# Stages of 256 tokens that begin on features not yet divided by their rms

## The chip, the cores and the metric

The kernel runs on one core of a Trainium2 chip. The metric is the device time of one execution in microseconds (us). Times are given of the profiled execution where a trace is read, and as medians where kernels are compared.

## The reference

A first block of two layers works on 256 tokens `x` and, in its first layer, on 256 context tokens as well; a second block of two layers works on the 256 tokens alone. The width is 1024. Every stage begins with an rms norm over the 1024 features of a token, times a weight that is put together from the norm's gain and a scale, plus a shift:

```python
def rms_norm_2(x, g):
    xf = x.astype(jnp.float32)
    y = xf * lax.rsqrt(jnp.mean(xf * xf, axis=-1, keepdims=True) + EPS)
    return (y * g.astype(jnp.float32)).astype(x.dtype)

def modulate_2(x, shift, scale):
    return x * (1 + scale[:, None, :]) + shift[:, None, :]

def sqrelu_mlp(hn, w1, w2):
    return jnp.square(jax.nn.relu(hn @ w1)) @ w2

def conv_ffn(h, w_up, conv_w, conv_b, w_down):      # first block
    a = h @ w_up
    a = lax.conv_general_dilated(a, conv_w, ...) + conv_b     # 3 taps, per feature
    gate, val = jnp.split(a, 2, axis=-1)
    return (jax.nn.silu(gate) * val) @ w_down

def second_block(x, c, ...):
    h = x
    for layer in range(DEPTH):
        sh1, sc1, g1, sh2, sc2, g2 = ...
        hn = modulate_2(rms_norm_2(h, norm1_g[layer]), sh1, sc1)
        y = recurrent_mixer(hn, ...) if layer < N_A_LAYERS else chunk_attention(hn, ..., k_pad, v_pad)
        h = h + g1[:, None, :] * y
        hn = modulate_2(rms_norm_2(h, norm2_g[layer]), sh2, sc2)
        h = h + g2[:, None, :] * sqrelu_mlp(hn, mlp_w1[layer], mlp_w2[layer])
        if layer == N_A_LAYERS - 1:
            k_pad, v_pad = shared_kv(h, c_act, ...)  # keys and values, from a norm of their own
    return h
```

## The kernel before

**Layout.** Activations lie with features on the partitions: `x` is 8 tiles (`KD`) of 128 features by 256 tokens (`T`), and a matrix of weights is used as blocks of 128 by 128. A product of fp32 precision is made of three fp32r matmuls in `mm3` (lines 338 to 340): both operands are split into a high and a low part, and wh·hi, wh·lo and wl·hi are summed in PSUM. `load_w` (line 306) brings a block of 128 by 1024 weights: SP issues the DMA into `st`, ACT casts the high part `wh` (line 311), DVE subtracts for the low part `wl` (line 315). `st`, `wh` and `wl` turn in 6 buffers, so the cast of the seventh block waits until TensorE has finished with the first.

**Order.** The program is written as Python code that a scheduler puts in order, by priorities, for every engine but TensorE, whose order is that of the code. Each engine then works through its own list in order. What stands in a list is the same in every execution.

**The hand-offs.** Where one stage ends and the next begins on 256 tokens, the norm stands between. There are five such places behind the first layer, called H1 to H5 here: H1 from the output matrix of the mixer (`wo`) to the conv FFN (`ffn1`), H2 from its last sums (`da`) to the recurrent layer (`lru_layer`), H3 from that layer's last sums (`da`) to the first MLP (`mlp`), H4 from the MLP's last sums to the attention (`attn_layer`, whose first products are `dt`: keys, then queries, then values), H5 from the attention's output matrix (`db`) to the second MLP. At each of them:

1. As one of the 8 output tiles leaves PSUM, DVE adds it to `x` (line 472), ACT squares it (lines 400 and 404), DVE sums the squares (line 405).
2. After the last, TensorE sums over the partitions (`nps`, line 416), DVE takes the root in nine small steps (lines 419 and 289 to 302, up to `nbc`), and TensorE transposes the result (`npt`, line 426). A few matmuls without use (`warm`, line 274) stand in between.
3. `norm_k` (line 445) makes each of 8 tiles of normalised features: DVE `nt` = x times 1/rms (line 447), ACT the high part (line 448), ACT or DVE the same again unrounded (`nhf`, lines 451 and 453), DVE or POOL the low part (line 454). The parts are named by their stage: `h21h`, `h21l` at H1, `lhh`, `lhl` at H2, `m0h`, `m0l` at H3, `kvh`, `kvl` and `hqh`, `hql` at H4, `m1h`, `m1l` at H5.
4. `lead_b` (line 1205) runs four matrices at once through the 8 tiles, tile by tile, into banks `ld`: 96 matmuls. What follows takes a matrix at a time (`pair_b`, line 1216, `up` in the recurrent layer), into `up`.

**What comes of the products.** In the MLPs two matrices make one pair: `evac` (line 1253) takes Relu and square on ACT and the square's low part on DVE. The down matrices (`da`) begin six pairs behind (`LAG_MLP`), which here means after eight up matrices; they sum into four PSUM banks over the whole stage (`DownAcc`, line 495 on), the last three (`LAG_MLP[1]`) held back and run one output tile after another. In `ffn1` a pair is gate and value of the conv FFN (`glu`, line 1076), and `da` begins after five pairs. In the recurrent layer `sink_x` (line 1320) makes the conv, `xh` on ACT (line 1327), `xl` on POOL (line 1328); the gates (`gt`) take these, and from them runs a long chain of ACT, DVE and POOL work and a scan.

## Time and profile before

| | before |
|---|---|
| median of 3 runs | 1752.1 us (1749.39 to 1755.54) |
| profiled execution | 1752.06 us, of which span 1750.3 us |
| TensorE busy | 1634.3 us (93%) |
| VectorE (DVE) busy | 1343.4 us (77%) |
| ScalarE (ACT) busy | 888.1 us (51%) |
| GpSimd (POOL) busy | 179.6 us (10%) |
| chain of waits, share by engine | PE 71%, DVE 8%, ACT 3% |

PE is the matmuls, PEld TensorE's loads of weights, which overlap them. A matmul's own duration is longer than its share of a dense stream, since matmuls overlap; the pace is read from one start to the next. A granted clock of 1.00 is full speed. In a timeline row the bracket gives the idle time of the engine ahead of the instruction, and what ended it. The execution lasts 1.8 us longer than its span.

### The profile page before, as it was taken

To read this page: it belongs to the slowest core of one execution; us is meant where nothing else is said; L and a number is where in the kernel's file an instruction comes from. 1 tells how busy PE (TensorE), PEld (TensorE's weight loads), DVE (VectorE), ACT (ScalarE), POOL (GpSimd) and SP (SyncE) were. 2 spreads that over 40 slices of the span, in tenths; PEclk is the share of its full clock that TensorE was granted. 3 is DMA by queue.
4 is the path that set the end of the run, shared out by engine and by line. 5 is a ranking of instruction groups with operands and counts; after the bars stand their busy time and mean duration, and the time that the engine had idled before them with its cause. 6 is when DMAs were issued, how large, how long until landed. Compare 5 with 4: busy or idle time off the path is not lost.

```text
span 1750.3 us, 28553 instructions
## 1 busy us (share of the span) xinstructions
PE 1634.3 (93%) x10850; PEld 1413.9 (81%) x10850; DVE 1343.4 (77%) x2589; ACT 888.1 (51%) x1526; POOL 179.6 (10%) x247
## 2 busy tenths in 40 slices
PE   6997989999999998987999998897999999899999
PEld 3774459888888886844899997896999977499999
DVE  5868757689999957876689777887888887668553
ACT  4537555542333435565565555765544464655442
POOL 2220220000000001102000001432000011400000
PEclk9999989999999998998899998998999989999999
DMA  9316436246878533152557553456888843668552
GB/s 335 105 48 218 169 124 209 102 138 199 273 224 312 187 111 101 61 181 108 181 197 249 184 180 104 129 180 198 291 318 323 299 152 121 217 241 277 187 186 73
DMA packets 91354, 327.91 MB, mean 187 GB/s; under 512 B 10064, under 2 KB 11088, under 8 KB 90704
## 3 DMA queue, kind: packets, MB, share of 16 engines
q1 hardware_dynamic: 90928, 323.99, 54.7%
q0 software_dynamic: 288, 2.10, 0.3%
q8 instruction: 85, 1.39, 0.3%
q14 instruction: 53, 0.43, 0.1%
HBM read 325.00 MB, written 1.05 MB: 186 GB/s over the span
## 4 chain that ended last, share of the span: by engine, by line
PE 71%; DVE 8%; ACT 3%; issue 3%; POOL 2%; DMA 1%; POOLq 0%; DVEq 0%; ACTq 0%
PE up L339 10%; PE up L338 10%; PE up L340 10%; PE da L338 5%; PE da L339 5%; PE da L340 5%; DVE wl L315 3%; PE dn L338 2%; PE dn L340 2%; PE dn L339 2%; PE dt L544 2%; PE dt L542 2%; PE dt L543 2%; PE opb L648 1%; PE gv L353 1%
## 5 line engine op out<-in xcount | busy, mean ns | idle before, releaser
L311 ACT CAST wh<-st 128x1024 fp32r<-128x1024 f32 (+3 forms) x392 | 401.2, 1030 | 449.7 <-PE up L339 173.4
L315 DVE TENSOR_TENSOR wl<-st,wh 128x1024 fp32r<-128x1024 f32 (+3 forms) x392 | 470.5, 1207 | 139.8 <-ACT wh L311 132.8
L386 DVE CUSTOM_DVE_ANT_0 gst<-gst,crow,cols 128x1024 f32<-128x1024 f32 x128 | 163.6, 1283 | 31.2 <-DMA gst<-in_ada21t_dram 14.4
L338 PE MATMUL up<-h2h,wh 128*128 128x512 f32 (+1 forms) x384 | 143.3, 373 | 1.7 <-ACT h2h L448 1.2
L340 PE MATMUL up<-h2h,wl 128*128 128x512 f32 (+1 forms) x384 | 143.0, 372 | 1.3 <-DVE wl L315 1.3
L338 PE MATMUL da<-g2h,wh 128*128 128x256 f32 x512 | 144.1, 281 | 0.0
L339 PE MATMUL da<-g2l,wh 128*128 128x256 f32 x512 | 144.1, 281 | 0.0
L340 PE MATMUL da<-g2h,wl 128*128 128x256 f32 x512 | 144.1, 281 | 0.0
L339 PE MATMUL up<-h2l,wh 128*128 128x512 f32 (+1 forms) x384 | 143.0, 372 | 0.1
L339 PEld LDWEIGHTS da<-g2l,wh 128*128 128x128 f32 x512 | 96.7, 189 | 0.0
L340 PEld LDWEIGHTS da<-g2h,wl 128*128 128x128 f32 x512 | 96.7, 189 | 0.0
L338 PEld LDWEIGHTS da<-g2h,wh 128*128 128x128 f32 x512 | 96.7, 189 | 0.0
L339 PE MATMUL up<-h21l,wh 128*128 128x256 f32 x320 | 90.1, 281 | 0.0
L340 PE MATMUL up<-h21h,wl 128*128 128x256 f32 x320 | 90.0, 281 | 0.0
L338 PE MATMUL up<-h21h,wh 128*128 128x256 f32 x320 | 90.0, 281 | 0.0
L338 PEld LDWEIGHTS up<-h2h,wh 128*128 128x128 f32 x384 | 72.4, 188 | 15.0 <-ACT h2h L448 1.5
L340 PEld LDWEIGHTS up<-h2h,wl 128*128 128x128 f32 x384 | 72.4, 189 | 14.4 <-DVE wl L315 1.9
L339 PEld LDWEIGHTS up<-h2l,wh 128*128 128x128 f32 x384 | 72.4, 189 | 12.8 <-DVE h2l L454 0.3
L353 PE MATMUL gv<-gst,cst 128*32 128x512 f32 x320 | 59.1, 617 | 20.9 <-DMA gst<-in_w_ada_dram 16.2
L641 POOL TENSOR_SCALAR pf<-pf,rc 128x512 f32<-128x512 f32 (+2 forms) x80 | 43.1, 551 | 195.7 <-DVE rc L959 129.8
L340 PE MATMUL up<-m0h,wl 128*128 128x256 f32 x224 | 63.1, 282 | 0.0
L338 PE MATMUL up<-m1h,wh 128*128 128x256 f32 x224 | 63.0, 281 | 0.0
(542 smaller groups left out, 4780.2 us busy)
## 6 DMA issues: line engine op xcount, KB each, us to landing
st<-in_mlp_dram SPq DMA_DIRECT2D x128, 512.0 KB, 4.5
gst<-in_w_ada_dram SPq DMA_DIRECT2D x96, 512.0 KB, 4.4
st<-in_w_up_dram SPq DMA_DIRECT2D x88, 512.0 KB, 4.4
st<-in_w_in_dram SPq DMA_DIRECT2D x32, 512.0 KB, 3.6
gst<-in_ada20t_dram SPq DMA_DIRECT2D x32, 512.0 KB, 5.1
gst<-in_ada_dram SPq DMA_DIRECT2D x32, 512.0 KB, 4.4
gst<-in_ada21t_dram SPq DMA_DIRECT2D x32, 512.0 KB, 6.2
st<-in_w_down_dram SPq DMA_DIRECT2D x25, 512.0 KB, 3.6
```

Of the source, the lines that this page charges most:

```text
L311: S.copy(hi[:, :n], st[:, :n])
L315: eng.tensor_tensor(lo[:, :n], st[:, :n], f(hi[:, :n]), ALU.subtract)
L338: TE.matmul(ps, lhsT=wh, rhs=ah, start=first, stop=False, **kw)
L339: TE.matmul(ps, lhsT=wh, rhs=al, start=False, stop=False, **kw)
L340: TE.matmul(ps, lhsT=wl, rhs=ah, start=False, stop=last, **kw)
L353: TE.matmul(ps[32 * t:32 * t + 32, :], lhsT=cst[:, 2 * q + i, :], rhs=st[:, i * 512:i * 512 + 512], start=(q < 2), stop=(q >= 2), tile_pos ...
L386: V.tensor_tensor_reduce(o, st, r, 0.5, bias[:, b:b + 1], ALU.mult, ALU.add, dest[:, v, b:b + 1])
L542: TE.matmul(o, lhsT=hh[:, k, js], rhs=wh[:, wsl], start=(k == 0), stop=False)
L543: TE.matmul(o, lhsT=hh[:, k, js], rhs=wl[:, wsl], start=False, stop=False)
L544: TE.matmul(o, lhsT=hlo[:, k, js], rhs=wh[:, wsl], start=False, stop=(k == KD - 1))
L641: G.tensor_scalar(ap, ap, r[:, qt:qt + 1], 0.0, ALU.mult, ALU.add)
L648: TE.matmul(o[c, :], lhsT=vs[x](kt), rhs=PT[:, x, kt].rearrange("p a b -> p (a b)"), start=(kt == 0), stop=(kt == nkt - 1), tile_position= ...
```

## The change

A class `Ahead` takes the place of the norm at the five hand-offs. As an output tile leaves PSUM, ACT writes x times the weight of the norm, `xgh`, and DVE its low part `xgl`; the squares are summed on POOL. TensorE goes straight on to the four first matrices of the next stage with these. The operand has two more columns (258 in place of 256) that hold the shift, so that the product of the matrix and the shift comes out in column 256. `nps` stands between tiles 3 and 4 of the lead, `npt` between tiles 6 and 7 (`RSTD_AT`). ACT copies the transposed 1/rms to `rb`. As a matrix leaves PSUM (`leave`), DVE copies the shift's product (`ldc`) and multiplies the rest by 1/rms (`ldu`); ACT adds the one to the other (`full`, or as the bias of the MLP's Relu, which then takes 256 columns twice in place of 512 once). The two matrices behind the lead (numbers 4 and 5, `AHEAD`) are done in the same way (`more`). `norm_k` still makes all 8 tiles, for the matrices behind those; the warm matmuls of these hand-offs are gone.

At H4 the first half of the keys is made from `xgh` with the tokens on the output's partitions, so 1/rms is a number for each partition there; the shift's product comes from eight small matmuls `gv` on the raw weights, and one more that sums and spreads it. Besides, the sums of a stage lie otherwise in the banks (output tile m in bank m % 4), the tiles leave in the order 0 to 7, the MLPs hold back two down matrices in place of three, and the output goes out in other parts. The core of the diff:

```diff
-OUT_PARTS = ((0, 2, 4, 6), (1, 3, 5), (7,))
+OUT_PARTS = ((0, 1, 2, 3), (4, 5, 6), (7,))
...
-LAG_MLP = (6, 3)
+LAG_MLP = (6, 2)
+AHEAD = 6
+RSTD_AT = (4, 7)
...
+    class Ahead:
+        def __init__(self, x, gs, sh, norm_step=None):
+            self.x, self.gs, self.sh = x, gs, sh
+            self.sums = Sums(G)
...
+        def add(self, k):
+            hi, lo = [t[:, k, 0:T] for t in self.h]
+            S.activation(hi, self.x[:, k, :], AF.Identity, scale=self.gs[:, k:k + 1])
+            V.scalar_tensor_tensor(lo, self.x[:, k, :], self.gs[:, k:k + 1], f(hi), ALU.mult, ALU.subtract)
+            self.sums.add(self.x[:, k, :])
+
+        def lead(self, ws, hi, lo, offset=TAIL_PRIO):
+            bs = [da_bank(j) for j in range(4)]
+            for k in range(KD):
+                if k == RSTD_AT[0]:
+                    with tc.high_priority(offset=TAIL_PRIO):
+                        r = Rstd(self.sums.parts)
+                if k == RSTD_AT[1]:
+                    with tc.high_priority(offset=TAIL_PRIO):
+                        pt = r.done()
+                        self.rb = tl("rb", [T], F32, None, 1, "xg")
+                        S.copy(self.rb, pt)
+                self.mm(k, ws, bs)
+            us = [self.leave(b) for b in bs]
+            with tc.high_priority(offset=offset):
+                for k in range(KD):
+                    norm_k(k, self.x[:, k, :], self.rb, self.gs, self.sh, hi(k), lo(k))
+            return us
...
+        def leave(self, b):
+            with tc.high_priority(offset=PRIO):
+                c = st_("ldc", [1])
+                V.tensor_copy(c, b[:, T:T + 1])
+                u = tl("ldu", [T], F32, "ldu", 4, "xg")
+                V.tensor_tensor(u, b[:, 0:T], self.rb, ALU.mult)
+            return u, c
+
+        def full(self, uc):
+            S.activation(uc[0], uc[0], AF.Identity, bias=uc[1])
+            return uc[0]
...
         def ps(self, m):
-            return self.bk[m // 2][:, m % 2, :]
+            return self.bk[m % 4][:, m // 4, :]
...
-                for m in (0, 2, 4, 6, 1, 3, 5, 7):
+                for m in range(KD):
...
         def make(m):
             if m == 0:
-                ws = [load_w(I["mlp1"][layer, j]) for j in range(4)]
-                for j, b in enumerate(lead_b(ws, hi, lo, norm_step)):
+                us = ahead.lead([load_w(I["mlp1"][layer, j]) for j in range(4)], hi, lo)
+                for j in range(2):
                     with tc.high_priority(offset=LEAD_PRIO):
-                        evac(2 * j, b)
+                        evac(2 * j, us[2 * j:2 * j + 2])
             if m not in parts:
-                evac(m, pair_b([load_w(I["mlp1"][layer, m + j]) for j in range(2)], hi, lo))
+                ws = [load_w(I["mlp1"][layer, m + j]) for j in range(2)]
+                evac(m, ahead.more(ws) if m < AHEAD else pair_b(ws, hi, lo))
...
+        ka = keys_ahead()
+        next(ka)
         norms(gk, kvm[:, 0:8], kv)
-        blk(0, kv, post_kq("kn2", 0))
+        blk(1, kv, post_kq("kn2", 1), ka)
         norms(gq, mod[:, 0:8], hq)
-        blk(1, kv, post_kq("kn2", 1))
```

TensorE's list at H5, from the last product of the attention's output to the first of the MLP. Before:

```order
L340 MATMUL db<-mx2h,wl 128x256
L416 MATMUL nps<-ones_78,acc 128x2 x6
L274 MATMUL warm<-wz 128x256 x2
L426 MATMUL npt<-kc,nbc 128x128 x2
L274 MATMUL warm<-wz 128x256 x3
L338 MATMUL ld<-m1h,wh 128x256
```

TensorE's list at the same place now, around `npt` (four banks `da` of the lead in place of `ld`):

```order
L342 MATMUL da_16816<-xgh,wl 128x258
L340 MATMUL da_16817<-xgh,wh 128x258
L341 MATMUL da_16817<-xgl,wh 128x258
L342 MATMUL da_16817<-xgh,wl 128x258
L428 MATMUL npt<-kc,nbc 128x128 x2
L340 MATMUL da_16814<-xgh,wh 128x258
L341 MATMUL da_16814<-xgl,wh 128x258
```

The lead no longer stands behind `npt`; 84 of its 96 matmuls, which read `xgh` and `xgl`, stand ahead of it.

ACT's list at H5, around the last tiles of normalised features (`m1h`, `nhf`). Before, the last of them, the Relu of the lead (`mr`), its square (`g2h`) and the next weights:

```order
L448 ACTIVATE m1h<-nt,n_91,gs 128x256
L451 ACTIVATE nhf<-nt,n_91,gs 128x256
L448 ACTIVATE m1h<-nt,n_91,gs 128x256
L451 ACTIVATE nhf<-nt,n_91,gs 128x256
L311 CAST wh<-st 128x1024
L1257 ACTIVATE mr<-ld 128x512 x2
L1258 ACTIVATE g2h<-mr 128x512 x2
L311 CAST wh<-st 128x1024 x5
```

Now, from the second Relu of the lead to the last tile of normalised features:

```order
L1323 ACTIVATE mr<-ldu,ldc 128x256
L1326 ACTIVATE g2h<-mr 128x512
L453 ACTIVATE nhf<-nt,n_91,gs 128x256
L313 CAST wh<-st 128x1024 x2
L450 ACTIVATE m1h<-nt,n_91,gs 128x256
L313 CAST wh<-st 128x1024
L450 ACTIVATE m1h<-nt,n_91,gs 128x256
L453 ACTIVATE nhf<-nt,n_91,gs 128x256
L450 ACTIVATE m1h<-nt,n_91,gs 128x256
L453 ACTIVATE nhf<-nt,n_91,gs 128x256
L313 CAST wh<-st 128x1024
L450 ACTIVATE m1h<-nt,n_91,gs 128x256
```

The normalised tiles stood ahead of everything that the lead leaves behind; now they stand behind the lead's Relu and squares, and between six casts of weights.

ACT's list at H2, up to the first inputs of the gates (`xh`; `xv` is the conv's first tap, `ldu` what left the lead). Before:

```order
L451 ACTIVATE nhf<-nt,n_90,gs 128x256
L311 CAST wh<-st 128x1024
L1323 ACTIVATE xv<-ld,cols 128x256
L311 CAST wh<-st 128x768
L311 CAST wh<-st 128x1024
L311 CAST wh<-st 128x768
L311 CAST wh<-st 128x1024
L1323 ACTIVATE xv<-ld,cols 128x256 x2
L1327 CAST xh<-xv 128x256 x2
```

Now:

```order
L492 COPY rb<-npt 128x256
L313 CAST wh<-st 128x1024
L525 ACTIVATE ldu<-ldu,ldc 128x256 x4
L1385 ACTIVATE xv<-ldu,cols 128x256 x4
L313 CAST wh<-st 128x768
L313 CAST wh<-st 128x1024
L450 ACTIVATE lhh<-nt,n_90,gs 128x256
L313 CAST wh<-st 128x768
L313 CAST wh<-st 128x1024
L1389 CAST xh<-xv 128x256 x4
```

The first `xh` stood behind all 8 normalised tiles (`lhh`); now it stands behind one of them, and seven follow it.

## Rows read from the trace of the kernel before

**Rows 1.** The page: busy time of engines, then the chain by engine.

```profile
PE 1634.3 (93%) x10850; PEld 1413.9 (81%) x10850; DVE 1343.4 (77%) x2589; ACT 888.1 (51%) x1526; POOL 179.6 (10%) x247
...
PE 71%; DVE 8%; ACT 3%; issue 3%; POOL 2%; DMA 1%; POOLq 0%; DVEq 0%; ACTq 0%
```

**Rows 2.** Stretches: length, busy time (count) by engine, granted clock, DMA share, GB/s.

```profile
860.60:867.70 7.10, 5.41 (x26) 4.25 (x26) 5.20 (x17) 2.66 (x5) 0.00 (x0) 0.70 0.78 254
867.70:880.40 12.70, 12.70 (x98) 12.61 (x97) 4.27 (x10) 6.48 (x13) 2.94 (x4) 0.90 0.18 74
...
1056.00:1064.40 8.40, 5.28 (x26) 4.22 (x25) 6.63 (x20) 3.52 (x8) 0.00 (x0) 0.82 0.41 127
...
1212.00:1219.80 7.80, 5.29 (x25) 4.29 (x25) 7.33 (x18) 3.75 (x6) 0.00 (x0) 0.69 0.79 240
...
1404.00:1413.40 9.40, 6.97 (x27) 5.32 (x25) 7.50 (x19) 4.62 (x8) 0.00 (x0) 0.62 0.46 172
1413.40:1429.00 15.60, 14.76 (x57) 11.22 (x56) 10.94 (x19) 11.27 (x19) 3.19 (x4) 0.90 0.31 101
1558.00:1563.90 5.90, 4.03 (x26) 3.15 (x24) 4.42 (x15) 1.96 (x3) 0.00 (x0) 1.00 0.66 233
1563.90:1575.90 12.00, 11.91 (x97) 11.57 (x97) 5.05 (x13) 7.20 (x14) 2.95 (x4) 1.00 0.28 107
1575.90:1587.30 11.40, 11.40 (x99) 11.40 (x98) 11.29 (x13) 9.73 (x14) 0.00 (x0) 1.00 0.75 238
```

**Rows 3.** Timeline of PE at H1, H3 and H5: start, duration, instruction.

```profile
860.54 0.28 PE L340 MATMUL wo<-mixac,wl 128*128 128x256 f32 x1
...
897.47 0.28 PE L338 MATMUL da<-g1h,wh 128*128 128x256 f32 x1
...
1211.74 0.28 PE L340 MATMUL da<-yh,wl 128*128 128x256 f32 x1
...
1244.99 0.28 PE L338 MATMUL da<-g2h,wh 128*128 128x256 f32 x1
...
1557.80 0.28 PE L340 MATMUL db<-mx2h,wl 128*128 128x256 f32 x1
...
1587.27 0.28 PE L338 MATMUL da<-g2h,wh 128*128 128x256 f32 x1
```

**Rows 4.** Timeline of DVE at H5: two `nt`, five `wl`.

```profile
1568.15 0.74 DVE L447 TENSOR_TENSOR nt<-xres,npt 128x256 f32<-128x256 f32 x2
...
1579.57 5.76 DVE L315 TENSOR_TENSOR wl<-st,wh 128x1024 fp32r<-128x1024 f32 x5
```

**Rows 5.** Timeline of ACT at H5, in order of time.

```profile
1570.40 0.59 ACT L451 ACTIVATE nhf<-nt,n,gs 128x256 f32<-128x256 f32 x1
1574.93 1.05 ACT L311 CAST wh<-st 128x1024 fp32r<-128x1024 f32 x1 [3.93 <-PE ld L339]
1575.88 1.08 ACT L1257 ACTIVATE mr<-ld 128x512 f32<-128x512 f32 x2
...
1577.89 4.84 ACT L311 CAST wh<-st 128x1024 fp32r<-128x1024 f32 x5
```

**Rows 6.** Timeline of POOL at H5: the low part of the last tile.

```profile
1571.07 0.74 POOL L454 TENSOR_TENSOR m1l<-nhf,m1h 128x256 fp32r<-128x256 f32 x1 [1.24 <-ACT nhf L451]
```

**Rows 7.** Timeline of PE at H2: the first gates and the matrix behind them.

```profile
1082.10 0.58 PE L338 MATMUL gt<-xh,wh 128*128 128x256 f32 x1 [2.91 <-ACT xh L1327]
...
1085.68 0.58 PE L339 MATMUL gt<-xl,wh 128*128 128x256 f32 x1 [1.03 <-POOL xl L1328]
...
1087.56 0.41 PE L338 MATMUL up<-lhh,wh 128*128 128x256 f32 x1
```

**Rows 8.** Timeline of PE at H4: first queries, and where they wait.

```profile
1438.75 0.40 PE L542 MATMUL dt<-wh,hqh 128*128 128x512 f32 x1
1438.98 0.39 PE L543 MATMUL dt<-wl,hqh 128*128 128x512 f32 x1
...
1450.95 0.50 PE L544 MATMUL dt<-wh,hql 128*128 128x512 f32 x1 [1.77 <-POOL hql L454]
```

More of the change, by code (lines that the diff above doesn't have):

```diff
@@ L554, in head_norm @@
         n = nh * d
-        for t in range(2):
-            S.copy(z[:, t], bks[t][:, c0:c0 + n])
+        if bks:
+            for t in range(2):
+                S.copy(z[:, t], bks[t][:, c0:c0 + n])
         sq = tl("zsq", [2, n], F32, "ztmp", bufs, "d")
@@ L1256, in evac @@
             r = tl("mr", [2, T], F32, "mr", 2, "f")
-            S.activation(r, b, AF.Relu)
+            if isinstance(b, list):
+                for y, (u, c) in enumerate(b):
+                    S.activation(r[:, y], u, AF.Relu, bias=c)
+            else:
+                S.activation(r, b, AF.Relu)
             S.activation(g[0], r, AF.Square)
@@ L1373, in up @@
             w = load_w(I["lru_in"][1, m])
+            if m < AHEAD:
+                sink_x(m, ahead.full(ahead.more([w])[0]))
+                return
             b = bank("up")[:, :T]
@@ L1380, in lru_layer @@
         ws = [load_w(I["lru_in"][1, j]) for j in range(4)]
-        for j, b in enumerate(lead_b(ws, hi, lo, norm_step)):
-            for y in range(2):
-                with tc.high_priority(offset=LEAD_PRIO):
-                    sink_x(2 * j + y, b[:, y])
+        for j, u in enumerate(ahead.lead(ws, hi, lo, 0)):
+            with tc.high_priority(offset=LEAD_PRIO):
+                sink_x(j, ahead.full(u))
         gate = dense_b(lambda m: I["lru_in"][0, m], LRU_K, KD, hi, lo, T, sink_g)
         acc = DownAcc(LRU_K, LRU_LAGS[2])
-        sink = resid_sink(x, mod[:, 16:24], accs)
+        sink = resid_sink(x, mod[:, 16:24], nxt)
         for m in range(LRU_K + LRU_LAGS[1]):
@@ L1398, in lru_layer, with attn_layer @@
         tap("xl", x)
-    def attn_layer(x, accs, mod, kvm, late):
-        gk = gs_of(col("kvg"), kvm[:, 8:16])
+    def attn_layer(x, ahead, mod, kvm, late, nxt):
+        gk = ahead.gs
         gq = gs_of(col("n1h1"), mod[:, 8:16])
@@ L1414, in norms, with keys_ahead @@
             for k in range(KD):
-                norm_k(k, x[:, k, :], rb, g, sh, h[0][:, k, :], h[1][:, k, :])
+                norm_k(k, x[:, k, :], ahead.rb, g, sh, h[0][:, k, :], h[1][:, k, :])
+        def keys_ahead():
+            bks = [bank("dt") for j in range(2)]
+            gv = pools["ps"].tile([P, 512], F32, name="gv", tag="gv", bufs=1)
+            ws = []
+            for k in range(KD):
+                if k % 2 == 0:
+                    ws.append(load_w(I["kvq"][0, k // 2], raw=True))
+                if k == RSTD_AT[0]:
+                    with tc.high_priority(offset=TAIL_PRIO):
+                        r = Rstd(ahead.sums.parts)
+                if k == RSTD_AT[1]:
+                    with tc.high_priority(offset=TAIL_PRIO):
+                        pt = r.done()
+                        ahead.rb = tl("rb", [T], F32, None, 1, "xg")
+                        S.copy(ahead.rb, pt)
+                wh, wl = [w[:, k % 2 * 512:k % 2 * 512 + 512] for w in ws[-1][:2]]
+                for j in range(2):
+                    hi, lo = [t[:, k, j * P:(j + 1) * P] for t in ahead.h]
+                    TE.matmul(bks[j], lhsT=hi, rhs=wh, start=(k == 0), stop=False)
+                    TE.matmul(bks[j], lhsT=hi, rhs=wl, start=False, stop=False)
+                    TE.matmul(bks[j], lhsT=lo, rhs=wh, start=False, stop=(k == KD - 1))
+                if k % 4 == 3:
+                    for kk in range(k - 3, k + 1):
+                        t = 32 * (kk % 4)
+                        TE.matmul(gv[t:t + 32, :], lhsT=ksh[:, kk, :],
+                                  rhs=ws[kk // 2][2][:, kk % 2 * 512:kk % 2 * 512 + 512], start=(kk < 4), stop=(kk >= 4),
+                                  tile_position=(0, t), skip_group_check=True)
+            sp = tl("shp", [512], F32, None, 1, "d")
+            S.copy(sp, gv)
+            yield
+            pt = tbank("shb")
+            TE.matmul(pt, lhsT=wz[:, 0:P], rhs=sp, start=True, stop=True)
+            sb = tl("shb", [512], F32, None, 1, "d")
+            S.activation(sb, pt, AF.Copy, scale=1.0 / 32)
+            zk = z["kn2", 0] = tl("z2", [2, 512], F32, "z2", 4, "m")
+            for t in range(2):
+                V.scalar_tensor_tensor(zk[:, t], bks[t], r.bc[:, t, 0:1], sb, ALU.mult, ALU.add)
+            head_norm(None, 0, 8, 64, [(0, 8, row("kn2"), None)], zk)
+            yield
```

144 lines of the change are left out of this document (80 added, 64 removed).

## Prediction

> **What bounds the kernel now.** The page comes first: PE is busy for 1634.3 of 1750.3 us, and the chain that ends last runs on PE for 71% [rows 1]. So what counts is the time in which PE has nothing to do or runs slowly. The table of stretches shows where the change can reach it [rows 2]. At each of the five hand-offs PE does no product of the program for 7.1, 8.4, 7.8, 9.4 and 5.9 us (H1 to H5; its busy time there is the sums, the transposes and the warm matmuls). Behind that a lead of 96 matmuls takes 12.7 us at H1 (granted clock 0.90) and 12.0 us at H5 (1.00), where the next 96 take 11.4 us, or 0.119 us each. At H4 the first block takes 15.6 us for what its pace of 0.233 us [rows 8] would do in 11.2. The most that could be won is these 38.6 us of gaps and some 6 us of slow leads, about 45 us.
>
> The third view is the list of each engine: what must a hand-off do before the next long stream of PE runs freely? Before, that is quickly answered: all 8 normalised tiles are made in one piece, ACT's last `nhf` of H5 starts at 1570.40, the low part of the last tile starts on POOL at 1571.07 [rows 5, 6], and from the start of the lead on PE waits for nothing more; the first `da` starts 29.47 us after the last `db` started, and 36.93 us and 33.25 us are the like times at H1 and H3 [rows 3]. Times below are counted from that last matmul of the old stage.
>
> **H5, step by step.** On PE: the lead starts at 0.1 in place of 6.1. Its 96 matmuls cost 11.4 us as before; the 2 more columns of 256 are 0.1 us. `nps` and `npt`, 14 matmuls that lay in the gap, now lie in the stream: the 26 instructions of the gap are busy for 4.03 us [rows 2], so I take 2 us. The lead ends at 13.4 (before: 18.1), and matrices 4 and 5 at 19.1. The root on DVE has the 4.2 us of tiles 4 to 6 to itself; before it fitted, with the sums, the transposes and the first tile, into 5.9 us. So far PE is 4.7 us ahead.
>
> Then come matrices 6 and 7, and these need the normalised tiles. `rb` exists only at 12.5, since `npt` stands behind tile 6. From there ACT has, up to the `nhf` of tile 7 (the list of the change, and its rows ahead of the piece shown): 6 casts at 0.97 (4.84 for 5) = 5.8 us; 8 high parts and 5 `nhf` at 0.5 = 6.5; four Relu of 256 columns at 0.4 (an estimate: 0.54 for 512) = 1.6; two squares at 0.55 = 1.1; together 15.0 us [rows 5]. The first cast can't start before the lead has freed its buffer, at 13.4: before, it waited 3.93 us for just that [rows 5]. DVE is tied in with it: its list has 3 of the 8 `nt` (0.37 each) behind what matrices 4 and 5 leave, which PE ends at 19.1, and three `wl` of 1.15 among them [rows 4]; by its own sum `nt` of tile 7 comes at 27.0, just when ACT asks for it. So the last `nhf` ends at 28.4, POOL's low part (0.74) at 29.2 [rows 6]. Matrix 6 ends at 29.5, matrix 7, 24 matmuls later, at 32.3, and `da` begins there: **2.9 us later than before**. Of the 13 us from 19.1 to 32.3 PE works for 5.7. What was won ahead of the norm is lost behind it, since the second pass of the norm is still made, later, and in a list that holds the casts and the Relu as well.
>
> **H1** is the same with more in the list: four `full` and four first taps at 0.5, two tanh and two casts at 0.4 on ACT, and twelve taps and products of 0.4 on DVE ahead of tile 2. The low part of tile 7 then comes at about 32.2, the pair that waits for it ends at 35.4, the pair behind it at 41.1; before 36.9: **4.2 us later**. **H3** has the list of H5, but two long gemv steps of DVE lie among those of the root, and the lead ends at 14.2: `da` at 33.1, before 33.25: **nothing**.
>
> **H2.** The gates need only the matrices of the lead. The first `xh` comes at about 24, two `gt` pairs end at 26.3; before, the first 12 `gt` ended at 31.7 (1087.56) after waits of 2.91 and 1.03 us [rows 7]. But matrix 6 needs all normalised tiles, which follow on ACT between the conv, the gates' tanh and two casts: 37.8, and its end at 38.0; before, 66 matmuls behind 1087.56 it ended at about 39.6. Of the 5.4 us that the gates are ahead I keep **1.5**.
>
> **H4.** Keys start at 0.1; 48 matmuls at 0.233 = 11.2, the eight `gv` and `nps`, `npt` 3 to 4 us, the second half of the keys on normalised tiles 12: both done at 28.9 in place of 34.84, where the first query started [rows 8]. The queries then need their own 8 tiles: 25.5 us of ACT from `rb` on, so about 40.5, and POOL's low part behind. Before, PE waited there 1.77 us, until 1450.95, which is 47.0 [rows 8]; now until 41.3 to 44. I take **3.5 us won**, within 2.5 to 5.5.
>
> **Work that is hidden.** ACT's `xgh` and square (0.9 us a tile) and DVE's `xgl` lie beside products of 2.85 us a tile at H1 and H5; at the other three a tile leaves every 0.7 us, so that tile 7 comes 1.5 us late, but PE wants it only at 11.5. The sums on POOL (5 steps at 0.74) are done before tile 4. Without that cover each would cost its own 0.4 to 0.9 us. The other output parts and the shorter tail move the last transfer by at most 0.5 us either way.
>
> **The clock.** The gap of H5 is granted 1.00, that of H1 0.70, and the lead behind H1 takes 0.7 us more than that behind H5 [rows 2]. The new waits at H1, H3, H4 and H5 are longer than those gaps (up to 11 us with little in them), and no warm matmul stands in them. I take 1.0 us for each, 4 us in all; bounds are 0 (as at H5) and 1.3 us (12.7 against 11.4) for each 96 matmuls behind it. The Trainium skill (Perfetto Trace Analysis, Matmul Optimizations) says that TensorE scales its power with its use, so matmuls should run back to back in batches. By that rule the lead gains, since it now follows its predecessor without a gap, and matrices 6 and 7 lose; the gap of H1 bears it out, the one of H5 doesn't, and taken to the full it would make the 4 us about 5.
>
> **Sum:** 2.9 + 4.2 + 0 − 1.5 − 3.5 + 4.0 = +6.1 us on the profiled 1752.06, which is the median of the runs (1752.1) but for 0.04: **1758 us**. Bounds: ACT's 13 steps of the norm at H5 ran in 7.8 us for 6.5 of work, so lists that wait for each other may take 20% longer, 3 us at each of H1, H3 and H5: 1767. Without a slower clock and with 1 us less at H1 and H5: 1752.
>
> **Rivals.** *Not slower: what is ahead stays ahead.* The recurrent layer lives on the chain behind its gates, and attention on its keys; if the 5.4 us and 5.9 us are kept in full, and the clock costs nothing, the sum is 2.9 + 4.2 − 5.4 − 5.9 = −4.2, or with the casts at H1 and H5 done in ACT's idle time ahead of 13.4, −7: 1745 to 1748. For it: PE waits for the gates before [rows 7]. Against it: matrix 6 and the queries have waits of their own in the list.
> *Much faster: the normalised tiles are in time.* Then PE never stops behind the lead: H1 −6.5, H3 −7.6, H5 −4.7, H2 −5.4, H4 −5.9, together −30: 1722. Decided at 19.1 by tile 7; the sum of ACT alone speaks against it.
> *Slower still: every tile waits for two lists.* The 20% above, and 48 matmuls behind each wait at the lower of the two clocks: 1768.
> *The change doesn't do what it says:* the lead waits for `xgl` or a bank and starts no earlier; the time then rises by the waits alone, about 1760, inside the range.
>
> **How the numbers follow.** The forecast 0.50; ahead stays ahead 0.22; much faster 0.10; slower still 0.15; the lead not early 0.03. A measurement here tells 0.3%, 5.3 us, from no change: faster is below 1746.8, slower above 1757.4. The forecast's own spread, 1751 to 1766, puts 0.33 of its 0.50 above and 0.16 within, 0.01 below; the first rival 0.16 below and 0.06 within; the second 0.10 below; the last two 0.16 above and 0.02 within. Faster 0.27, same 0.24, slower 0.49. The range from 1741 to 1769 leaves out the second rival and a little of the slow end.
>
> **What would show it.** Right: in the new trace `da` of the four banks starts 0.1 us behind the last `db`, and `up` of the MLP waits some 8 to 10 us for `m1h`, `m1l` (ACT or POOL) around 20 to 29 us; the first queries start 5 us earlier and wait for `hql` longer than 1.77 us; the granted clock of these stretches is below 1. Wrong: no wait of `up` above 3 us; a lead that waits for `xgh`, `xgl` or for a bank; or the first `da` of H5 earlier than 29.5 us.

## The result and the profile after

The changed kernel takes **1774.9 us** in the median of 4 runs (1770.5 to 1780.1); the kernel before took 1751.9 us beside it. The ratio is **1.013, with a 95% interval from 1.009 to 1.017**. It is slower, as forecast, but by 23 us, where 6 were forecast; the time lies above the range. The profiled execution took 1780.1 us, with a span of 1778.3 us.

Busy time of the engines in the changed kernel (the page's first part, as in [rows 1]):

```profile
PE 1641.4 (92%) x10818; PEld 1414.5 (80%) x10818; DVE 1375.4 (77%) x2660; ACT 912.1 (51%) x1593; POOL 210.6 (12%) x272
```

TensorE's products are almost the same; the 28 us by which the span grew are time in which it stands or runs slowly. To see where, each hand-off is measured as in the prediction, from the start of the last matmul of the old stage. The layer is the recurrent layer, from the last `da` of the conv FFN to its own last `da`; H2 is told by the start of the twelfth gate product; H4 runs to the attention's first transpose, and "attention" from there to its first output product `db`. All are read from PE's timeline of one profiled execution each (us):

| kernel | H1 | H2, gates | layer | H3 | H4 | attention | H5 | that execution |
|---|---|---|---|---|---|---|---|---|
| before | 36.9 | 31.5 | 155.9 | 33.3 | 81.8 | 48.6 | 29.5 | 1752.1 |
| changed | 42.7 | 27.2 | 158.8 | 33.5 | 90.3 | 56.1 | 33.2 | 1780.1 |
| e10 (changed, again) | 42.7 | 27.2 | 158.8 | 33.5 | 90.3 | 50.2 | 32.9 | 1773.5 |
| e1 | 39.0 | 31.3 | 159.0 | 32.2 | 80.7 | 53.5 | 31.9 | 1759.6 |
| e2 | 42.7 | 27.2 | 158.7 | 25.3 | 87.8 | 49.4 | 24.8 | 1756.5 |
| e3 | 42.7 | 27.2 | 158.7 | 33.5 | 80.2 | 49.6 | 33.1 | 1761.4 |
| e4 | 42.4 | 27.2 | 158.9 | 38.7 | 89.3 | 48.3 | 38.2 | 1784.6 |
| e5 | 31.3 | 27.2 | 159.2 | 26.2 | 80.9 | 48.7 | 24.8 | 1741.8 |
| e6 | 42.7 | 26.0 | 158.8 | 34.9 | 87.3 | 50.4 | 33.3 | 1773.0 |
| e7 | 38.8 | 26.0 | 156.9 | 35.9 | 84.3 | 49.4 | 36.1 | 1764.5 |
| e8 | 31.3 | 35.2 | 161.8 | 25.5 | 80.1 | 49.2 | 24.8 | 1740.5 |
| e9 | 42.7 | 33.6 | 160.2 | 34.9 | 87.7 | 49.7 | 36.8 | 1772.1 |
| e11 | 31.3 | 33.5 | 158.6 | 25.7 | 79.9 | 50.1 | 24.8 | 1740.1 |
| e12 | 41.2 | 32.5 | 157.8 | 35.0 | 87.9 | 50.0 | 33.0 | 1770.2 |

From before to the changed kernel: H1 +5.8, the layer +2.9, H3 +0.2, H4 +8.5, attention +7.5, H5 +3.7; with −0.7 for the rest that is the 27.9 us between the last products of the two executions. In e10, the same kernel once more, every hand-off is the same to 0.3 us, and attention is 6 us shorter.

**H5** shows the shape that the prediction spoke of. TensorE's timeline in the changed kernel (start, duration, instruction, and in the bracket its idle time and what ended it), where [rows 3] has it before:

```profile
1581.95 0.28 PE L342 MATMUL db<-mx2h,wl 128*128 128x256 f32 x1
1582.07 0.28 PE L340 MATMUL da<-xgh,wh 128*128 128x258 f32 x1
...
1595.16 0.28 PE L340 MATMUL up<-xgh,wh 128*128 128x258 f32 x1
...
1602.54 0.39 PE L342 MATMUL up<-m1h,wl 128*128 128x256 f32 x1 [1.19 <-DVE wl L317]
...
1606.03 0.38 PE L341 MATMUL up<-m1l,wh 128*128 128x256 f32 x1 [1.34 <-DVE m1l L456]
...
1608.08 0.58 PE L341 MATMUL up<-m1l,wh 128*128 128x256 f32 x1 [1.43 <-POOL m1l L456]
...
1610.42 0.58 PE L341 MATMUL up<-m1l,wh 128*128 128x256 f32 x1 [0.69 <-POOL m1l L456]
...
1615.17 0.28 PE L340 MATMUL da<-g2h,wh 128*128 128x256 f32 x1
```

The lead starts 0.12 us behind the last `db` and waits for nothing. Then matrix 6 waits, once for the low part of its weights (1.19 us) and then tile by tile for the normalised features; with one short wait that is not shown, the five sum to 5.0 us. ACT's list there, where [rows 5] has it before:

```profile
1593.98 0.37 ACT L492 COPY rb<-npt 128x256 f32<-128x256 f32 x1 [8.85 <-PE npt L428]
1594.24 1.06 ACT L313 CAST wh<-st 128x1024 fp32r<-128x1024 f32 x1
...
1601.75 1.98 ACT L313 CAST wh<-st 128x1024 fp32r<-128x1024 f32 x2
1603.64 0.60 ACT L450 ACTIVATE m1h<-nt,n,gs 128x256 fp32r<-128x256 f32 x1
1604.14 1.03 ACT L313 CAST wh<-st 128x1024 fp32r<-128x1024 f32 x1
...
1608.85 0.59 ACT L453 ACTIVATE nhf<-nt,n,gs 128x256 f32<-128x256 f32 x1
```

From `rb` to the last `nhf` ACT never rests for more than 0.2 us: the stage waits for the sum of ACT's list.

**H4** is another matter. TensorE's waits at the first queries, and ACT's timeline beside them, where [rows 8] has PE before:

```profile
1448.10 0.80 PE L616 MATMUL dt<-wh,hql 128*128 128x512 f32 x1 [4.46 <-DVE hql L456]
...
1458.55 0.50 PE L614 MATMUL dt<-wh,hqh 128*128 128x512 f32 x1 [1.64 <-ACT hqh L450]
...
1463.12 0.79 PE L616 MATMUL dt<-wh,hql 128*128 128x512 f32 x1 [1.00 <-POOL hql L456]
...
1468.18 0.50 PE L616 MATMUL dt<-wh,hql 128*128 128x512 f32 x1 [0.15 <-POOL hql L456]
```

```profile
1449.72 0.60 ACT L450 ACTIVATE hqh<-nt,n,gs 128x256 fp32r<-128x256 f32 x1 [3.04 <-DVE nt L449]
1452.77 1.05 ACT L313 CAST wh<-st 128x1024 fp32r<-128x1024 f32 x1 [2.45 <-PE dt L616]
1453.72 0.60 ACT L450 ACTIVATE hqh<-nt,n,gs 128x256 fp32r<-128x256 f32 x1
...
1456.95 1.04 ACT L313 CAST wh<-st 128x1024 fp32r<-128x1024 f32 x1 [2.13 <-PE dt L616]
1457.90 0.60 ACT L450 ACTIVATE hqh<-nt,n,gs 128x256 fp32r<-128x256 f32 x1
1460.13 0.60 ACT L450 ACTIVATE hqh<-nt,n,gs 128x256 fp32r<-128x256 f32 x1 [1.63 <-DVE nt L449]
...
1465.23 1.04 ACT L313 CAST wh<-st 128x1024 fp32r<-128x1024 f32 x1 [2.96 <-PE dt L616]
```

Here ACT does rest: 12.2 us in these five waits. Three times a cast of weights stands and waits until TensorE has read its buffer, while the next `hqh`, for which TensorE waits, stands behind that cast in ACT's list. The two engines go round in a circle, a tile at a time. The clock takes part in it: behind the 4.46 us in which TensorE stood, its granted clock is 0.50, the lower of its two levels (length, busy time with count of PE, PEld, DVE, ACT, POOL, granted clock, DMA share, GB/s):

```profile
1448.10:1453.40 5.30, 5.30 (x13) 4.14 (x14) 4.93 (x13) 1.23 (x2) 0.00 (x0) 0.50 0.43 138
```

At the pace of 0.233 us, 13 products take 3.0 us; and as long as TensorE reads a buffer, the cast that wants it waits. How much of H4 the clock makes varies between kernels: e2, e4, e9 and e12 leave the lists of ACT, DVE and POOL from the last `da` to the first transpose as they are in the changed kernel, instruction for instruction, and H4 is 87.8, 89.3, 87.7 and 87.9 there, with a granted clock of 0.94 in the first 60 us of e2 and e9 in place of 0.89.

### The profile page after: what moved, and what is told of

Read it like the earlier page. It is cut to its first block, busy times and chain, and to the rows that moved or that the text cites. A ratio compares the mean times of both kernels' runs of the same rounds, so it can differ in the third digit from the quotient of the medians.

```text
span 1778.3 us, 28664 instructions
## 1 busy us (share of the span) xinstructions
PE 1641.4 (92%) x10818; PEld 1414.5 (80%) x10818; DVE 1375.4 (77%) x2660; ACT 912.1 (51%) x1593; POOL 210.6 (12%) x272
## 5 line engine op out<-in xcount | busy, mean ns | idle before, releaser
L341 PE MATMUL up<-h21l,wh 128*128 128x256 f32 x304 | 87.8, 289 | 4.1 <-DVE h21l L456 3.4
L340 PE MATMUL up<-h21h,wh 128*128 128x256 f32 x304 | 87.7, 288 | 2.1 <-ACT h21h L450 2.0
L341 PEld LDWEIGHTS up<-h2l,wh 128*128 128x128 f32 x384 | 72.3, 188 | 12.9 <-DVE h2l L456 0.3
L407 POOL TENSOR_TENSOR acc<-acc,sq 128x256 f32<-128x256 f32 x25 | 21.9, 876 | 386.1 <-issue 330.9
L341 PE MATMUL up<-m1l,wh 128*128 128x256 f32 x208 | 60.0, 289 | 3.8 <-POOL m1l L456 2.4
```

The source lines that it names most:

```text
L340: TE.matmul(ps, lhsT=wh, rhs=ah, start=first, stop=False, **kw)
L341: TE.matmul(ps, lhsT=wh, rhs=al, start=False, stop=False, **kw)
L407: self.eng.tensor_tensor(self.parts[0], self.parts[0], sq, ALU.add)
```

## The experiments

**e1: the second pass of the norm ahead of the rest.** At all hand-offs the normalised tiles get a priority far above casts, Relu and conv.

```diff
-            with tc.high_priority(offset=offset):
+            with tc.high_priority(offset=3000):
                 for k in range(KD):
                     norm_k(k, self.x[:, k, :], ...)
...
         def norms(g, sh, h):
-            for k in range(KD):
-                norm_k(k, x[:, k, :], ahead.rb, ...)
+            with tc.high_priority(offset=3000):
+                for k in range(KD):
+                    norm_k(k, x[:, k, :], ahead.rb, ...)
```

> The changed kernel with one thing moved: the second pass of the norm (nt, high part, nhf, low part) gets a far higher priority, at the four hand-offs that end in a matrix product and for keys and queries at H4, so that it stands ahead of the casts of weights in the lists of ACT and DVE; nothing is left out. Theory (the tiles queue behind casts, and at H4 a cast waits for a buffer that PE frees only with the next tile): the last tile comes 4 to 5 us earlier, the first da 38 us behind the last wo at H1 (42.7 in the changed kernel), 29 to 30 at H3 and H5 (33.5, 33.2), the first transpose of the attention 80 us behind the last da at H4 (90.3); together about 20 us less than the changed kernel, 1751 to 1755. Rival (the clock: PE is slow behind the waits whatever their length): under 8 us less. Rival (the work added in the lead, its leaves and shift columns): within 4 us of the changed kernel.

1759.3 us, ratio to before 1.0034 (1.0024 to 1.0045): 16 us of the loss are gone. H4 falls from 90.3 to 80.7, so the order of the list makes that loss, with the waits and the slow clock that come of it (the edit doesn't part these two); TensorE's last wait there ends 46.0 us behind the old stage, in place of 55.6:

```profile
1444.61 0.50 PE L616 MATMUL dt<-wh,hql 128*128 128x512 f32 x1 [0.76 <-DVE hql L456]
...
1451.76 0.50 PE L616 MATMUL dt<-wh,hql 128*128 128x512 f32 x1 [0.56 <-POOL hql L456]
```

H3 and H5 miss what was expected by some 2 us each, and the total by 4. The wait only changed its name: the casts now stand behind the norm, and matrix 6 waits once for weights, at H3:

```profile
1239.90 0.58 PE L342 MATMUL up<-m0h,wl 128*128 128x256 f32 x1 [5.17 <-DVE wl L317]
```

**e2: no normalised tiles in the MLPs.** All 32 up matrices run on the undivided features, and the norm's second pass is left out there.

```diff
-                evac(m, ahead.more(ws) if m < AHEAD else pair_b(ws, hi, lo))
+                evac(m, ahead.more(ws))
```

> The changed kernel with all 32 up matrices of both MLPs on the undivided features, so that the MLPs make no normalised tiles at all; each matrix leaves PSUM as those of the lead do. Theory: nothing waits for tiles at H3 and H5, the first da starts 25 to 27 us behind the last da or db (33.5 and 33.2 in the changed kernel), about 14 us less than the changed kernel in all, 1757 to 1760. Rival (the leaves and the halved Relu are the cost): 28 more of them in each MLP, so the same time or up to 10 us more than the changed kernel.

1756.3 us, ratio 1.0025 (1.0012 to 1.0038). H3 is 25.3 and H5 24.8 us, both below before, and the stream behind each takes 160.1 us in place of 158.9. The waits for the normalised tiles and the norm's work were the whole price at H3 and H5. (H4 is 2.6 us shorter too, with its lists unchanged; see the clock there.)

**e3: H4 as before.** The keys start on normalised tiles again, with the warm matmuls.

```diff
-        ka = keys_ahead()
-        next(ka)
+        with tc.high_priority(offset=TAIL_PRIO):
+            r = Rstd(ahead.sums.parts)
+            warm(WARM[1])
+            pt = r.done()
...
-        blk(1, kv, post_kq("kn2", 1), ka)
+        blk(0, kv, post_kq("kn2", 0))
...
+        blk(1, kv, post_kq("kn2", 1))
```

> The changed kernel with H4 alone as before the change: norm first, warm matmuls, both halves of the keys on normalised tiles, the sums of that norm on DVE. Theory: the first transpose of the attention comes 81 to 82 us behind the last da again (90.3 in the changed kernel), so about 8 us less than the changed kernel. Rival (H4 only shows what the attention behind it would lose anyway, or its loss is a transfer that comes late): under 3 us less.

1766.9 us, ratio 1.0086 (1.0065 to 1.0107): 8 us less than the changed kernel. H4 is 80.2.

**e4: warm matmuls in the new waits.** Four stand ahead of each of tiles 1 to 7 in the first pair that waits, at H1, H3 and H5.

```diff
+                if first and j == 0 and k:
+                    for _ in range(4):
+                        TE.matmul(wb, lhsT=wz[:, 0:P], rhs=wz, start=True, stop=True)
```

> The changed kernel with 4 matmuls without use ahead of each tile but the first, in the first matrix that takes normalised tiles at H1, H3 and H5, where PE waits. Rival (the clock is the cost): the granted clock stays at 1.00 there and the first da comes 4 to 5 us earlier at H1 and 2 to 3 at H3 and H5, 8 to 11 us less in all. Theory (the lists are the cost): the tiles come as late as before, the first da at most 2 us earlier at H1 and 1 at H3 and H5: 0 to 4 us less.

1785.7 us, ratio 1.0181 (1.0161 to 1.0201): 11 us more than the changed kernel, which neither expected. Stretches at H1 and H3 up to the last wait and behind it (length; busy time with count of PE, PEld, DVE, ACT, POOL; granted clock; DMA share; GB/s), first of the changed kernel:

```profile
883.00:891.00 8.00, 4.16 (x13) 2.71 (x13) 8.00 (x18) 7.31 (x14) 2.00 (x3) 0.53 0.29 83
891.00:903.00 12.00, 12.00 (x78) 12.00 (x79) 9.84 (x15) 6.44 (x12) 0.49 (x1) 0.74 0.76 269
1241.00:1249.20 8.20, 4.11 (x21) 3.21 (x21) 8.20 (x15) 7.84 (x13) 4.41 (x3) 0.76 0.58 182
1249.20:1253.70 4.50, 4.50 (x27) 4.50 (x28) 4.50 (x6) 1.58 (x2) 0.00 (x0) 0.67 0.93 250
```

and of e4:

```profile
885.50:893.40 7.90, 7.90 (x44) 7.12 (x43) 7.90 (x18) 7.21 (x14) 1.67 (x3) 1.00 0.32 77
893.40:905.40 12.00, 12.00 (x93) 11.66 (x92) 10.52 (x16) 7.05 (x12) 0.82 (x1) 1.00 0.85 293
1243.90:1258.10 14.20, 14.20 (x74) 12.78 (x75) 14.20 (x22) 8.16 (x14) 4.09 (x3) 1.00 0.70 214
1258.10:1261.50 3.40, 3.40 (x29) 3.36 (x28) 1.04 (x3) 1.05 (x1) 0.00 (x0) 1.00 0.99 358
```

The clock is cured: granted 1.00 throughout. But at H3 and H5 the warm matmuls fill more than the waits. In a row of e4 it reads

```profile
1244.12 1.89 PE L1287 MATMUL warm<-wz 128*128 128x256 f32 x8
1245.66 0.47 PE L340 MATMUL up<-m0h,wh 128*128 128x256 f32 x1
```

that is 1.54 us from start to start, seven times, 10.8 us, in place of waits that sum to 4.9 us there. H1, where the waits (6.2 us) and the slow clock cost more, comes out even (−0.3); H3 and H5 lose 5.2 and 5.0. The run shows at the same time what the clock costs in the changed kernel: from the start of the last waiting product to the first `da` at H1 77 matmuls take 12.0 us, at H3 and H5 26 take 4.5 and 4.75; in e4 as many take 9.3, 3.3 and 3.3 (75 in 9.06 and 27 in 3.38 and 3.37, at their pace). So the slow clock costs 2.7, 1.2 and 1.5 us behind the waits.

**e5: everything ahead.** The conv FFN, the MLPs and the recurrent branch run all their up matrices on undivided features; H4 as in e3. The recurrent layer's gate branch still has normalised tiles.

```diff
-            elif p == 2:
-                ready.update(zip((4, 5), ahead.more(...)))
+            elif p >= 2:
+                ready.update(zip((2 * p, 2 * p + 1), ahead.more(...)))
...
-            if m < AHEAD:
+            if m < LRU_K:
                 sink_x(m, ahead.full(ahead.more([w])[0]))
```

> All products of both MLPs, of the conv FFN and of the recurrent branch on the undivided features, so that H1, H3 and H5 have no second pass of the norm and at H2 only the gate branch takes normalised tiles; H4 as before the change. Theory: H1 falls to about 31 us (first da behind the last wo; 42.7 in the changed kernel, 36.9 before), H3 and H5 to 25 (as with the MLPs alone), H4 to 80, and the recurrent stage, now without a wait for tiles at matrix 6, to 154 to 157 us (158.8 in the changed kernel, 155.9 before); in all 1733 to 1742, faster than before the change. Rival (DVE and ACT, which take 2 leaves more for each pair, become the bound of the conv FFN): the FFN from first to last da rises from 158.5 by more than 6 us and eats what H1 gains; 1745 or more.

**1740.4 us, ratio to before 0.9932 (0.9914 to 0.9949): faster than both kernels.** H1 is 31.3, H3 26.2, H5 24.8; the three streams behind cost 1.8, 1.2 and 1.2 us more. The layer, expected at 154 to 157, stays at 159.2: matrix 6 no longer waits for a tile there, and nothing is won by it.

**e6: seven buffers for the weights, five for what comes from memory.**

```diff
-W_REST = (6, 6)
+W_REST = (5, 7)
```

> The changed kernel with seven buffers for the two parts of a weight block in place of six, and five in place of six for the raw weights. Theory (at H4 a cast of weights waits for a buffer that PE frees with the next tiles, and those tiles stand behind the cast): each such cast waits for one block less, and the first transpose of the attention comes 84 to 87 us behind the last da (90.3 in the changed kernel). Rival (H4 loses by the sheer sum of ACT and DVE work): 89 us or more.

H4 is 87.3, 3.0 us less, at the edge of what the theory expected; it is a single execution. The circle is still there: three casts wait 5.7 us in all for TensorE, in place of 7.5. That the buffer is worth 3.0 us is not shown: e2, e9 and e12 have six buffers and the lists of the changed kernel at H4, and come to within 0.7 us of the same time.

**e7: the transpose `npt` one tile earlier.**

```diff
-RSTD_AT = (4, 7)
+RSTD_AT = (4, 6)
```

> The changed kernel with the transposes of the root one tile earlier in the lead (between tiles 5 and 6 in place of 6 and 7). Theory: 1/rms is there 1.4 us earlier, but the first cast behind it still waits for the end of the lead (the buffer it needs), and the casts stay in the list; the first da at H1, H3 and H5 comes 0 to 1 us earlier. Rival (the late 1/rms is what makes the tiles late): 1.4 us or more earlier at each. The root takes 2.0 us on DVE, two tiles 2.8 us on PE, so PE should not wait for it.

1764.5 us in a single execution; neither theory. H1 is 3.9 us shorter, H4 6.1, the layer 1.9, but H3 is 2.4 and H5 2.8 longer. 1/rms itself moved little (at H3 `npt` now waits 1.31 us for DVE); the scheduler put the lists of ACT and DVE in another order, and that moved every hand-off by several us, either way. At H5 matrix 6 waits 7.25 us for one `m1l`, a step on POOL that takes 7.39 us there and at most 2.09 in the changed kernel.

**e8 and e9: H2 as before**, in e5 and in the changed kernel. The four matrices of the lead stay in four banks.

```diff
-        for j, u in enumerate(ahead.lead(ws, hi, lo, 0)):
+        bs = [da_bank(j)[:, 0:T] for j in range(4)]
+        for k in range(KD):
+            norm_k(k, x[:, k, :], rb, ...)
+            for w, b in zip(ws, bs):
+                mm3(b, w[0][:, kk], w[1][:, kk], hi(k), lo(k), k == 0, k == KD - 1)
+        for j, b in enumerate(bs):
             with tc.high_priority(offset=LEAD_PRIO):
-                sink_x(j, ahead.full(u))
+                sink_x(j, b)
```

> e5 with the hand-off H2 as before (sums on DVE, warm matmuls, all eight normalised tiles ahead of the lead). Theory: the recurrent layer is paced by a chain of eleven scans of some 10 us each on DVE's list, so a lead that starts early gives nothing there (first scan at 44.1 us in the changed kernel, 44.3 before), and the extra instructions of the early start lengthen the list; with the old hand-off the last scan is back at 139 us, the layer at 156 to 157.5 us in place of 159.2, and the whole kernel at 1737 to 1739 us. Rival: what is lost there is lost at the layer's end, where each output tile now has the extra parts to make for the next stage; then the layer stays at 158.5 or more and the whole at 1740 or more, since the gap at H2 comes back as well.

> The changed kernel with H2 alone as before. Theory: the layer at 156 to 157.5 us in place of 158.8; the first twelve gates end at 31 to 32 in place of 27.2; the other stages as in the changed kernel (H1 42.7, H3 33.5, H4 up to the first transposes 90, H5 33.2). Rival (loss at the layer's end): 158.5 or more. The stretch from the attention's first transposes to the first output product was 56.1 us in the changed kernel's profile and 48 to 50 in most others: if the change's lists cause it, it is 55 to 57 here, if a late transfer of one execution does, 48 to 51.

e8: 1742.3 us, ratio 0.9946 (0.9928 to 0.9964). The layer got longer, to 161.8 and 160.2 us. The theory's size is refuted; the rival named the layer's end, and there little changed (last `yl` to last `da` is 6.9 us in e9 and 7.9 in e8, 7.0 before). The loss is at the start: first scan at 47.9 and 47.3, before 44.3. ACT's list was not that of before. All four first taps stand ahead of the casts, with twelve conv steps of DVE behind them, and later a cast waits for TensorE with the gates' tanh behind it (ACT, e9):

```profile
1076.91 1.93 ACT L1391 ACTIVATE xv<-da,cols 128x256 f32<-128x256 f32 x4
...
1090.01 1.04 ACT L313 CAST wh<-st 128x1024 fp32r<-128x1024 f32 x1 [6.16 <-PE gt L341]
```

Four banks let four outputs leave at once, and the scheduler did so. This and e10 also settled the attention: 49.7 and 50.2 us. The other hand-offs of e9 were to be as in the changed kernel. H1 was; H3 is 1.4 us longer, H4 2.6 shorter, and H5 is 36.8 in place of 33.2, with the same lists. One step of POOL made most of that, first in e9, then the same step in e12:

```profile
1595.05 7.30 POOL L456 TENSOR_TENSOR m1l<-nhf,m1h 128x256 fp32r<-128x256 f32 x2 [3.53 <-ACT nhf L453]
...
1596.62 1.77 POOL L456 TENSOR_TENSOR m1l<-nhf,m1h 128x256 fp32r<-128x256 f32 x1 [2.24 <-ACT nhf L453]
```

The first of the two in e9 takes 6.61 us, in which DVE works for 6.03, and matrix 6 waits 5.72 us for it. Before, where DVE had nothing to do beside it, such a step took 0.74 us [rows 6].

**e10: the changed kernel again.**

> The changed kernel once more, for a second profile. All hand-offs as in the first to 0.5 us. The stretch from the attention's first transposes to its first output product: 48 to 51 us and a total of 1767 to 1773 if the 56.1 of the first profile was one execution's late transfer; 55 to 57 and 1775 to 1781 if it belongs to the kernel.

Everything but attention is the same. In the first execution a transfer came late (PE, changed kernel), in the second less so (PE, e10):

```profile
1522.93 1.92 PE L355 MATMUL gv<-gst,cst 128*32 128x512 f32 x4 [3.63 <-DMA gst<-in_ada_dram]
```

```profile
1520.50 1.05 PE L355 MATMUL gv<-gst,cst 128*32 128x512 f32 x4 [1.45 <-DMA gst<-in_ada_dram]
```

Behind that wait the granted clock fell, and the next 42 products took 9.44 us in place of 5.35 (changed kernel, then e10):

```profile
1522.93:1532.37 9.44, 9.44 (x43) 4.31 (x43) 2.77 (x15) 3.97 (x13) 2.19 (x6) 0.52 0.18 63
```

```profile
1520.50:1525.85 5.35, 5.35 (x42) 2.65 (x43) 2.48 (x14) 3.41 (x12) 1.67 (x4) 1.00 0.65 206
```

So some 6 us of the profiled execution belong to that execution: all waits for these transfers in the attention are 5.2 us in place of 2.9, and the slow clock behind the longest adds 4.1. The other runs of the changed kernel, 1770.5 to 1778.4, have no profile; whether they differ by the same transfer was not seen.

**e11 and e12: as e8 and e9, with the lead in two banks**, two matrices to a bank, as before.

```diff
-        bs = [da_bank(j)[:, 0:T] for j in range(4)]
+        bs = [da_bank(j).rearrange("p (a t) -> p a t", a=2) for j in range(2)]
...
-                mm3(b, w[0][:, kk], ..., k == 0, k == KD - 1)
+                mm3(bs[j // 2][:, j % 2], w[0][:, kk], ..., k == 0 and j % 2 == 0, k == KD - 1, skip_group_check=True)
```

> e8 with the four matrices of the recurrent layer's lead in two banks, two to a bank, as before, where e8 has them in four. ACT's list behind the last normalised tile is then the one of before again: one first tap, four casts of weights, two taps, the first xh; in e8 all four first taps and the conv steps that follow them on DVE stand ahead. Theory: the order of this list sets the first gates, and the pace of the scans behind them sets the layer; first twelve gates at 31 to 32 in place of 35.2, first scan at 44 to 45 in place of 47.9, layer at 155.5 to 157.5 in place of 161.8, whole kernel at 1736 to 1739. Rival: the stage loses because the stages around it changed (its own end makes parts for the next stage, and its start shares DVE with the sums), so the layer stays above 159 and the whole at 1740 to 1743.

> e9 with two banks for that lead. Theory: first twelve gates at 31 to 32, layer 155.5 to 157.5 in place of 160.2 (e9) and 158.8 (the change); the other hand-offs as in e9 to 0.5 us. Rival: layer above 159.

e11: **1739.9 us, ratio 0.9923 (0.9904 to 0.9942)**; the layer is 158.6 us, 3.1 less than with four banks, and 157.8 in e12, 2.3 less. Both lie above what was expected (the gates by 1.5 and 0.5 us, the layer by 1.1 and 0.3) and below the rival's 159. The other hand-offs of e12 were expected as in e9; H1 is 1.4 us shorter and H5 3.8, with the same lists (at H1 the waits are the same 6.2 us, and the 77 products behind them take 10.5 us at a granted 0.86; at H5 it is the step of POOL shown above). The pace of the scans is that of before: in e12 94.9 us from the first scan to the last, in e11 94.6, before 94.6, each gap between two scans the same to 0.3 us in the three; 96.0 in e8 and e9, and 96.6 in the changed kernel. What is left is the start, and 1.1 us of that in e12 is the lead itself, which runs at a lower granted clock, first before, then e12:

```profile
1064.00:1077.00 13.00, 13.00 (x106) 12.82 (x105) 5.40 (x13) 7.75 (x15) 2.95 (x4) 0.97 0.01 3
```

```profile
1068.00:1081.00 13.00, 13.00 (x97) 12.82 (x96) 4.72 (x12) 6.74 (x13) 2.94 (x4) 0.87 0.00 2
```

It starts behind the old gap and the same warm matmuls in both. From its first start to its last the lead takes 11.6 us before, 11.9 in e9, 12.7 in e12 and 12.9 in e8 and e11; why the clock differs is open. e11 and e5 take the same time: at H2 the early lead is worth nothing, and the old start costs nothing.

## Why the prediction was right and wrong

The direction was right and its mechanism at H1, H3 and H5 held in the main; the size failed in two terms, H4 and H2, which were forecast as gains and came as losses.

- **H5, right.** Forecast: `rb` at 12.5, the last `nhf` ended at 28.4, first `da` at 32.3, and 1 us for the clock. Measured: 12.0, 27.5, 33.2. Adding up ACT's list worked, since ACT had no waits in it. But `up` waited 5.0 us there, not 8 to 10, and no single wait was above 1.43 us, where the prediction had called "no wait of `up` above 3 us" a sign of being wrong. The clock made part of the rest: the 26 products behind the last wait took 4.75 us at a granted 0.62.
- **H1, right in shape, 0.6 us short with its clock term** (+5.2 forecast, +5.8 measured). That it is so close is partly luck: the pair that waits was to have its last tile at 32.2 and had it at 30.7, and the clock took 2.7 us, not 1.0.
- **H3, right.** Forecast 33.1 and 1 us for the clock; measured 33.5.
- **The clock, right in kind, too small:** 4.0 us forecast for four places, 5.4 measured at three of them by e4; at H1 2.7 us for 77 matmuls, above the bound of 1.3 us for 96. The Trainium skill (Perfetto Trace Analysis, Matmul Optimizations) wants matmuls back to back; taken to the full, the prediction put it at about 5 us. The rows agree with the direction, and their 5.4 us leave H4 out. The Trainium skill (Perfetto Trace Analysis, Optimization Strategies) says that the goal is in general to keep the matmul engine's utilization as high as possible; busy time made of fillers is not that: e4 has PE busy in all of the stretch at H3 and takes 5.2 us longer there. The Trainium skill also says there to work on the engines that block the critical path, and e5, which takes work off ACT and DVE, is what paid.
- **H4, wrong, by 11 of the 15 us** between the forecast (1758) and the second execution (1773.5). The step that failed: "The queries then need their own 8 tiles: 25.5 us of ACT from `rb` on". It summed ACT's list as if ACT never waited. The last wait for `hql` ended at 55.6, not at 41.3 to 44; ACT's five waits there sum to 12.2 us. The clock's 1.0 us for H4 was too little as well: the lists of the changed kernel took 2.6 us less in e9, at a higher granted clock. The first query started at 30.3, near the 28.9 forecast: the keys were early, and it was the queries that lost it. The prediction had the circle in hand: it saw a cast wait 3.93 us for TensorE's buffer [rows 5], and used that only as a start time. Nor would the early keys have been worth 3.5 us: with the norm in time (e1), H4 is 80.7, 1.1 us less than before, and e3, e5, e8 and e11, with the old start of the keys, have 79.9 to 80.9.
- **H2, wrong, by 4.4 us.** The gates came 4.3 us earlier, as forecast (27.2; the step said about 26.3 for the end of two pairs). The step that failed is "Of the 5.4 us that the gates are ahead I keep 1.5": matrix 6 waited 3.20 us for `lhl` and ended at 40.1, not 38.0, and the layer does not end by matrix 6 anyway. It goes from scan to scan, eleven of them, 5 to 12 us apart and 9.5 on average, with DVE, ACT and POOL in turn. The first scan stood at 44.3 before and at 44.1 in the changed kernel: the head start was gone by then, and the last one came 1.8 us later:

```profile
1194.73 0.69 DVE L1370 TENSOR_TENSOR_SCAN xv<-w 128x256 f32<-128x256 f32 x1 [2.10 <-POOL w L1369]
```

```profile
1202.12 0.69 DVE L1432 TENSOR_TENSOR_SCAN xv<-w 128x256 f32<-128x256 f32 x1 [2.10 <-POOL w L1431]
```

  (the first of before, 138.8 us into its layer; the second of the changed kernel, 140.7). The remaining 1.1 us lie behind the last `yl`, where the output tiles leave. Why the scans between lose 2 us in the changed kernel is shown only so far: with the old list they don't (e12). Which instruction in the list does it stays open.
- **Attention, not in the sum.** It cost 1.5 us in e10 and 7.5 in the first profile. In the other runs with parts of the change it is 48.3 to 50.4, but for e1's 53.5, where the granted clock fell to 0.71 as well; so the late transfer is not the change's as far as these profiles can tell.
- **The rivals.** "Ahead stays ahead" fell with H2 and H4. "Slower still: every tile waits for two lists" was the right kind of mechanism at the wrong places: it was priced at H1, H3 and H5, where ACT hardly waited, and not at H4. Its 1768, near the upper end of the range, is also less than its own condition gives: 48 matmuls of 0.119 us at half the speed (granted 0.50, as the rows show it) are 5.7 us more behind each wait, which at four places, with the 9 us for the lists, makes over 1780. "Much faster" named −6.5, −7.6 and −4.7 us at H1, H3 and H5 if the normalised tiles were in time; without them e5 shows −5.6, −7.1 and −4.7 there, and gives 3.4 back in the layer and 4.2 in the longer streams.

## What to carry to other kernels

Summing an engine's list gives when its last item is done only if no item in it waits for the engine that waits for the list; where a ring of buffers ties a cast to TensorE's progress, and the tile TensorE needs stands behind that cast, each turn of the circle adds its own wait, and those must be added to the sum. Work that starts earlier is worth something only if the stage's own pace-setter starts earlier: look for the chain that repeats (here the scans) and see what its first link waits for. An early start that still needs the late version of its input for the rest of the stage only moves the gap; here it paid once nothing behind it needed that version. And the same lists can take 1 to 4 us more or less from one kernel to the next, by the granted clock or by one slow step: a difference of that size, at one place of one execution, is not yet the effect of an edit.
